# Attention values computed transposed in a hybrid decoder layer, with the reciprocal of the softmax sum spread along columns by transposes

## The chip, the cores and the metric

The kernel runs on one core of a Trainium2 chip. The metric is device time in microseconds of one execution; lower is better. Besides the time there is a profile of one execution. In it PE is TensorE's matmul side and PEld its weight loads, DVE is VectorE, ACT is ScalarE, POOL is GpSimd, and SP is SyncE, which issues most of the transfers.

## The reference

One layer of a decoder, on 512 tokens of 1024 features in float32, and a final RMS norm:

```python
h = rms_norm(x, ffn1_norm[l])
x = x + RES_HALF * swiglu(h, ffn1_w_gate[l], ffn1_w_up[l], ffn1_w_down[l])
h = rms_norm(x, mix_norm[l])
proj = h @ w_in[l]
u, q, k, v = jnp.split(proj, [D_SSM, D_SSM + D_ATTN, D_SSM + D_ATTN + D_KV], axis=-1)
q = partial_rope(...)                     # 8 heads of 64
k = partial_rope(...)                     # 2 heads of 64, v the same
y_ssm = s5_mixer(u, ...)                  # state space part, 512 features, ends in a GLU
y_attn = swa_sink_attention(q, k, v, attn_sinks[l])
y = jnp.concatenate([rms_norm(y_ssm, ssm_out_norm[l]),
                     rms_norm(y_attn, attn_out_norm[l])], axis=-1)
x = x + y @ w_out[l]
h = rms_norm(x, ffn2_norm[l])
x = x + RES_HALF * swiglu(h, ffn2_w_gate[l], ffn2_w_up[l], ffn2_w_down[l])
return rms_norm(x, final_norm)            # after the one layer
```

The attention works in four blocks of 128 tokens; a block sees its own keys and those of the block before it (the first block only its own), under a causal window of 128. Each head has a sink: one more logit in the softmax whose weight is left out of the sum over values.

```python
scores = jnp.where(mask[None, :, None, None], scores, NEG_INF)
probs = jax.nn.softmax(jnp.concatenate([scores, sink], axis=-1), axis=-1)[..., :-1]
out = jnp.einsum('bnkrqs,bnskd->bnqkrd', probs.astype(v.dtype), vw)
```

## The kernel before, in words

Activations are kept transposed: a tile has 128 features on the partitions and the 512 tokens along its columns, so `x` is eight tiles. The large products split weights and activations into a high part of the type fp32r and a rest (`hi`, `lo`), and `mm3` (L199 to L201) issues three matmuls of 512 columns for each pair: hi by hi, hi by lo, lo by hi. A weight arrives by DMA as `wraw`; ACT casts it to `whi` (L162) and DVE subtracts to get `wlo` (L190). The tiles for these three have three buffers each, which come free in the order in which the matmuls are done with them, and two weights are fetched ahead. RMS norms are applied late: a matmul with a column of ones sums the squares by token (`pr`, L244), DVE finds one over the root (`rsqrt`), and two matmuls of ones with two diagonal tiles `dg` (DVE, L265) spread it over the partitions (`prb`, L269); ACT copies that to `R` (L271). What a gained tile needs (`split_gain`) is one ACT op for `hi` (L212) and one DVE op for `lo` (L214).

The layer has three stages: a first feed-forward part, the mixing, and a second feed-forward part. The mixing is a list of steps. The string ORDER holds a letter and a number for each, and a loop runs them in that order; a scheduler then sets each engine's instructions, led by this order and by its own estimate of when inputs are ready. The string ENGINES says for some copies and element-wise operations on which engine they run; what it doesn't name has a default. The steps that matter here, with the tile of 128 tokens (or the half of the heads) as the number:

- `Q` transposes q of one block (`tq`) and makes `qT` from it: ACT the rounded part, and the rest (L1192) on the engine that ENGINES names under `ql`. Where that is POOL, ACT first copies the raw tile out (`qraw`).
- `S` makes the scores of half the heads of a block. DVE adds the mask and takes the row maximum (`mx`, L1394), then has three small operations of four columns: `m`, the maximum with the sink (L1399), `ng`, its negative (L1400), and `ds`, the sink less it (L1401).
- `E` exponentiates with `ng` as bias and the sum as a second result; `den` adds the sink's part, and `rec` is its reciprocal.
- `T` transposes the probabilities (`pt`, L1438), `V` computes the weighted values, `O` what the out-projection needs of them.
- `Y`, `Z`, `G`, `g`, `N0`, `D` are the state space output, its transposes, the GLU, the gate, the rms by token, and the split into `hi` and `lo`. `N1` is the spreading of its rms, named Rs below; `M0` and `M1` are the same for the attention, Ra below.
- `W` and `X` are the two halves of the out-projection (tile `ow`), eight output tiles each with 12 matmuls: `W` takes the state space features, `X` the attention's. `w` multiplies a `W` tile with Rs (`ot`, L1209) and adds it to `x` (L1210, POOL). `x` multiplies an `X` tile with Ra (L1216), adds it to `x` (L1217, DVE), and makes the gained tile for the second feed-forward part (L212, L214).

In `V` the values come out with tokens on the partitions: for each block, head and key block, the transposed probabilities (128 keys by 128 tokens) are the stationary operand and the 64 columns of the head's values are the moving one, so 56 fp32 matmuls (L1455) into `po`, 128 tokens by 8 heads of 64. DVE multiplies with `rec`, spread over a head's 64 columns by a broadcast access pattern, into `ya`; ACT sums its squares by token as a by-product, so that this rms takes no matmul. In `O` PE transposes `ya` (`ty`, L1468, four per block), and ACT and DVE make `ah` and `al`, 128 columns at a time (L1473, L1474).

## Time and profile before

| what | value |
|---|---|
| time, median of three runs (lowest to highest) | 905.81 us (904.67 to 906.43) |
| the profiled execution's own time | 905.8 us |
| its span in the profile | 903.9 us |
| mean granted TensorE clock | 0.996 |
| PE busy | 882.0 us, 98% |
| DVE, ACT, POOL busy | 693.4, 408.1 and 332.9 us |
| bytes moved by DMA | 100.38 MB |

How to read it: the span is the time from the first to the last recorded instruction of the core; the rest of the execution's own time lies around it. Busy times are sums over instructions. PE's is near the span throughout, but matmuls are pipelined and their ends are modelled, so a busy PE may still be waiting in part; what a stage is worth is read from the waits inside it. In rows of a timeline the first number is the start in microseconds from the span's start and the second the duration; a bracket at the end of a row tells how long the engine stood idle before it and what released it.

### The profile page before, as it was taken

How to read it: one execution, taken by the hardware profiler on the slowest of the kernel's cores; microseconds unless marked ns; L12 is line 12 of the kernel's file. 1: busy time of each engine (PE TensorE's matmuls, PEld its weight loads, DVE VectorE, ACT ScalarE, POOL GpSimd, SP SyncE). 2: the span in 40 equal slices, each digit the busy share in tenths (PEclk: the TensorE clock that was granted, in tenths of full speed). 3: DMA queues.
4: the chain of work that ended last, by engine and by line, in shares of the span. 5: the costliest groups of instructions: out<-in, count | busy, mean ns of one | idle time of the engine just before them, and what ended most of it. 6: DMA issues, size and time to landing. Idle time of an engine off the chain costs nothing. (4 is left out here: it accounts for less than half of the span.)

```text
span 903.9 us, 14334 instructions
## 1 busy us (share of the span) xinstructions
PE 882.0 (98%) x5396; PEld 773.7 (86%) x5396; DVE 693.4 (77%) x1253; ACT 408.1 (45%) x768; POOL 332.9 (37%) x295
## 2 busy tenths in 40 slices
PE   9999999999999999999989999999999999999996
PEld 6887888878998898788879887888999889988995
DVE  7998856786995595949887787796798569955966
ACT  7143333323653354612497443552455335533553
POOL 0235227925540450501332153290554055404502
PEclk9999999999999999999999999999999999999999
DMA  7421534455213524456201122223421442144112
GB/s 250 139 83 40 168 121 159 132 157 192 89 36 111 175 87 162 150 176 184 71 1 47 47 94 93 94 70 121 159 88 36 146 152 88 36 127 170 48 48 93
DMA packets 42116, 100.38 MB, mean 111 GB/s; under 512 B 8544, under 2 KB 10816, under 8 KB 41536
## 3 DMA queue, kind: packets, MB, share of 16 engines
q1 hardware_dynamic: 41616, 98.93, 33.9%
q8 instruction: 42, 0.69, 0.3%
q10 hardware_dynamic: 432, 0.55, 0.2%
q14 instruction: 26, 0.21, 0.1%
HBM read 91.63 MB, written 7.83 MB: 110 GB/s over the span
## 5 line engine op out<-in xcount | busy, mean ns | idle before, releaser
L162 ACT CAST whi<-wraw 128x1024 fp32r<-128x1024 f32 (+4 forms) x114 | 101.5, 899 | 210.3 <-PE dn L200 69.8
L190 DVE TENSOR_TENSOR wlo<-wraw,whi 128x1024 fp32r<-128x1024 f32 (+4 forms) x113 | 129.5, 1152 | 35.6 <-ACT whi L162 31.9
L199 PE MATMUL dn<-hi,whi 128*128 128x512 f32 (+1 forms) x336 | 127.5, 386 | 1.1 <-ACT whi L162 1.1
L200 PE MATMUL dn<-lo,whi 128*128 128x512 f32 (+1 forms) x336 | 127.9, 384 | 0.0
L201 PE MATMUL dn<-hi,wlo 128*128 128x512 f32 (+1 forms) x336 | 126.1, 384 | 1.6 <-DVE wlo L190 1.6
L562 POOL TENSOR_TENSOR s<-s,wraw 128x512 f32<-128x512 f32 x52 | 83.2, 1601 | 55.3 <-DVE x L448 35.5
L562 POOL TENSOR_TENSOR s<-wb 128x512 f32<-128x512 f32 x26 | 37.5, 1443 | 168.6 <-DMA wb<-wgs 167.8
L596 DVE TENSOR_TENSOR wlo<-s,whi 128x512 fp32r<-128x512 f32 x104 | 89.1, 898 | 13.2 <-ACT whi L595 12.7
L448 DVE SCALAR_TENSOR_TENSOR x<-dn,x 128x512 f32<-128x512 f32 x56 | 38.3, 688 | 74.0 <-PE dn L201 73.8
L595 ACT CAST whi<-s 128x512 fp32r<-128x512 f32 x104 | 59.3, 619 | 41.6 <-issue 14.9
L199 PE MATMUL gu<-hi,whi 128*128 128x512 f32 x192 | 74.7, 397 | 1.4 <-ACT hi L212 1.3
L199 PEld LDWEIGHTS dn<-hi,whi 128*128 128x128 f32 x336 | 63.1, 188 | 15.0 <-ACT whi L162 2.8
L201 PEld LDWEIGHTS dn<-hi,wlo 128*128 128x128 f32 x336 | 63.0, 188 | 14.5 <-DVE wlo L190 2.0
L200 PE MATMUL gu<-lo,whi 128*128 128x512 f32 x192 | 75.1, 393 | 0.2
L201 PE MATMUL gu<-hi,wlo 128*128 128x512 f32 x192 | 74.3, 390 | 0.0
L200 PEld LDWEIGHTS dn<-lo,whi 128*128 128x128 f32 x336 | 63.1, 188 | 12.1
L286 POOL TENSOR_TENSOR sq<-sq 128x512 f32<-128x512 f32 x17 | 26.0, 1528 | 69.9 <-ACT sq L282 69.8
L596 DVE TENSOR_TENSOR wlo<-wraw,whi 128x512 fp32r<-128x512 f32 x52 | 50.3, 999 | 0.0
L199 PEld LDWEIGHTS gu<-hi,whi 128*128 128x128 f32 x192 | 36.0, 189 | 10.3 <-ACT hi L212 2.0
L200 PEld LDWEIGHTS gu<-lo,whi 128*128 128x128 f32 x192 | 36.3, 189 | 8.8 <-DVE lo L214 1.7
L595 ACT CAST whi<-wraw 128x512 fp32r<-128x512 f32 x52 | 29.2, 615 | 30.0 <-PE dn L200 30.0
L201 PEld LDWEIGHTS gu<-hi,wlo 128*128 128x128 f32 x192 | 36.1, 188 | 7.5
(428 smaller groups left out, 2598.4 us busy)
## 6 DMA issues: line engine op xcount, KB each, us to landing
wraw<-wd SPq DMA_DIRECT2D x48, 384.0 KB, 3.2
wraw<-wgu SPq DMA_DIRECT2D x34, 512.0 KB, 3.5
wb<-wgs SPq DMA_DIRECT2D x52, 256.0 KB, 5.0
wraw<-wgs SPq DMA_DIRECT2D x26, 512.0 KB, 3.5
wraw<-wout SPq DMA_DIRECT2D x8, 512.0 KB, 3.5
x<-xT SPq DMA_DIRECT2D x8, 256.0 KB, 5.1
kV<-mV SPq DMA_DIRECT2D x8, 256.0 KB, 3.2
kC<-mC SPq DMA_DIRECT2D x8, 256.0 KB, 3.1
```

The costliest lines, as they stand in the source:

```text
L162: (e.copy if e is self.nc.scalar else e.tensor_copy)(out, x)
L190: self.eng("lo" + key).tensor_tensor(lo, raw, hi.bitcast(F32), op=ALU.subtract)
L199: mm(out, wh, xh, start=start, stop=False, **kw)
L200: mm(out, wh, xl, start=False, stop=False, **kw)
L201: mm(out, wl, xh, start=False, stop=stop, **kw)
L286: (eng or b.nc.gpsimd).tensor_tensor(self.acc, self.acc, sq, op=ALU.add)
L448: self.added = self.nc.vector.scalar_tensor_tensor(self.x[m], ps, 0.5, self.x[m], op0=ALU.mult, op1=ALU.add)
L562: add = lambda o, x, y: nc.gpsimd.tensor_tensor(o, x, y, op=ALU.add)
L595: self.chained("A", lambda: A.copy(hi[:, c], w))
L596: self.chained("V", lambda: V.tensor_tensor(lo[:, c], w, hi[:, c].bitcast(F32), op=ALU.subtract))
```

## The change

Six things change, all in the mixing stage.

1. **Values.** The values are now the stationary operand (128 keys by 64 features) and the transposed probabilities of two heads the moving one (256 columns), so the result `po` has features on the partitions and tokens along the columns. The heads of the first key-value head go to output rows 0 to 63, those of the second to rows 64 to 127. That is 28 matmuls (L1479 after the change) in place of 56. One `po` tile now holds half the heads of two blocks. The features come out in another order, so the rows of w_out and of the attention's gain are laid out in that order (`ha`) on the way in.
2. **One over the sum.** `rec` would now have to vary along columns. A copy on POOL spreads each block half's `rec` over 64 columns a head (`rx`, eight copies of 256 elements), PE transposes it (`rb`, L1468, four per block, in place of the four of `ya`), ACT copies the result out, and DVE multiplies it with `po` into `ya`, eight operations.
3. **What the out-projection needs.** `O` has no transposes; it makes `ah` and `al` 256 columns at a time, for two blocks at once. The squares (`sa`) are ACT operations of their own with DVE additions, and the rms by token takes eight matmuls with the column of ones, issued among the out-projection's matmuls.
4. **Row maximum.** `m` is gone: `ng` comes in one operation from `mx` and the negated sinks (made once ahead), and `ds` is the sink plus `ng`.
5. **Engines.** `ql1` and `ql3`, four `qT` operations, go from POOL to DVE, and their two `qraw` copies on ACT fall away.
6. **Order.** ORDER is a new one: among others O0 comes before V3 and takes the first two blocks, O1 after it the other two, M0 stands behind O1, N1 before M1, and M1 behind X1. A small tile that `warm_up` makes on POOL, which moves the addresses of the tiles behind it, has 16 columns instead of 32.

```diff
-        m, ng, ds = tiny("m"), tiny("ng"), tiny("ds")
-        V.tensor_tensor(m, mx, sink, op=ALU.max)
-        V.tensor_scalar(ng, m, -1.0, None, op0=ALU.mult)
-        V.tensor_tensor(ds, sink, m, op=ALU.subtract)
+        ng, ds = tiny("ng"), tiny("ds")
+        V.scalar_tensor_tensor(ng, mx, -1.0, self.nsinks[:, half * 4:half * 4 + 4], op0=ALU.mult, op1=ALU.min)
+        V.tensor_tensor(ds, sink, ng, op=ALU.add)
...
         if half == 0:
-            self.rec[b] = self.tp.tile([P, NH], F32, name="rec", bufs=4)
-        V.reciprocal(self.rec[b][:, half * 4:half * 4 + 4], den)
+            self.rec[b] = self.m2(name="rx")
+        rx = self.rec[b][:, half * 256:(half + 1) * 256]
+        self.copy(f"rx{i}", rx.rearrange("p (j v e) -> p v j e", j=2, v=2),
+                  rec.rearrange("p (v j o) -> p v j o", v=2, j=2).broadcast_to([P, 2, 2, HD]), "G")
...
     def values(self, b):
...
-        po = self.ps("po")
-        for n, h in enumerate(HEADS):
...
-                PE.matmul(po[:, n * HD:(n + 1) * HD], pt[:, c:c + P], self.v[:, k0 + kb, kv * HD:(kv + 1) * HD],
-                          start=(kb == 0), stop=(kb == nk - 1))
...
+        ps = self.ps("rb")
+        for k in range(4):
+            PE.transpose(ps[:, k * P:(k + 1) * P], self.rec[b][:, k * P:(k + 1) * P], self.ident)
+        rb = self.m2(name="rb")
+        self.nc.scalar.copy(rb, ps)
+        for half in range(2):
...
             for kb in range(nk):
...
+                for kv in range(2):
+                    pt = self.pts[2 * b + half][kv][:, :2 * nk * P].rearrange("p (j k q) -> p j k q", j=2, k=nk)
+                    PE.matmul(po[kv * HD:(kv + 1) * HD], self.v[:, k0 + kb, kv * HD:(kv + 1) * HD],
+                              pt[:, :, kb], start=(kb == 0), stop=(kb == nk - 1), skip_group_check=True)
+            V.tensor_tensor(ya, po, rb[:, half * 256:(half + 1) * 256].rearrange("p (j q) -> p j q", j=2), op=ALU.mult)
+
+    def attn_out(self, bp):
...
+                hi, lo = (a[:, bp * 256:(bp + 1) * 256] for a in self.attn[k])
+                y = ya[:, j * 256:(j + 1) * 256]
+                nc.scalar.activation(hi, y, AF.Copy, scale=g)
+                nc.vector.scalar_tensor_tensor(lo, y, g, hi.bitcast(F32), op0=ALU.mult, op1=ALU.subtract)
+            sq = self.m2(name="sa")
+            nc.scalar.activation(sq, ya, AF.Square)
```

Three places show how instructions move. Rows have the source line, the operation, output from inputs and the tile; line numbers after the change are a few higher. The first is PE between the last probability transposes and the out-projection (`L199 ow`, after the change `L200 ow`), before:

```order
L1438 MATMUL pt<-cst,pr 128x128 x8
L1455 MATMUL po<-v,pt 128x64 x8
L1438 MATMUL pt<-cst,pr 128x128 x8
L1455 MATMUL po<-v,pt 128x64 x8
L1468 MATMUL ty<-cst,ya 128x128 x4
L1455 MATMUL po<-v,pt 128x64 x4
L1438 MATMUL pt<-cst,pr 128x128 x8
L1455 MATMUL po<-v,pt 128x64 x20
L199 MATMUL ow<-hi,whi 128x512
L244 MATMUL pr<-cst,sq 128x1 x4
L1468 MATMUL ty<-cst,ya 128x128 x4
```

and after:

```order
L1456 MATMUL pt<-cst,pr 128x128 x16
L1468 MATMUL rb<-cst,rx 128x128 x4
L1479 MATMUL po<-pt,v 64x2x128
L1456 MATMUL pt<-cst,pr 128x128 x4
L1479 MATMUL po<-pt,v 64x2x128
L1456 MATMUL pt<-cst,pr 128x128 x12
L1479 MATMUL po<-pt,v 64x2x128 x3
L1468 MATMUL rb<-cst,rx 128x128 x4
L1479 MATMUL po<-pt,v 64x2x128 x11
L1456 MATMUL pt<-cst,pr 128x128 x8
L1468 MATMUL rb<-cst,rx 128x128 x2
```

The values are half as many and stand singly, in threes and in an eleven; the transposes between are of `rb` and come ahead of the values that they scale, where those of `ya` came behind them.

The second place is ACT around the two copies of a spread rms (`R<-prb`), of which the first is the attention's before the change and the state space part's after it. Before:

```order
L162 CAST whi<-wraw 128x1024
L1473 ACTIVATE ah<-ty,gains 128x128 x3
L162 CAST whi<-wraw 128x1024
L271 COPY R<-prb 128x512
L1473 ACTIVATE ah<-ty,gains 128x128
L271 COPY R<-prb 128x512
L162 CAST whi<-wraw 128x1024
L212 ACTIVATE hi<-x_90,gains 128x512
L282 ACTIVATE sq<-x_90 128x512
```

After:

```order
L1492 ACTIVATE ah<-ya,gains 128x256 x2
L1495 ACTIVATE sa<-ya 128x512
L163 CAST whi<-wraw 128x1024
L272 COPY R<-prb 128x512
L163 CAST whi<-wraw 128x1024 x3
L272 COPY R<-prb 128x512
L213 ACTIVATE hi<-x_90,gains 128x512
L283 ACTIVATE sq<-x_90 128x512
```

Three weight casts now stand between the two copies, none right behind the second, and the wider `ah` all stand ahead of the first.

The third is DVE at the same place, from the diagonals of the later spreading (`dg`) through the adds (`ot`, and `x`, whose first tile is x_90). Before:

```order
L265 TENSOR_TENSOR dg<-cst,rb_h 128x512
L265 TENSOR_TENSOR dg<-cst,rb_l 128x512
L190 TENSOR_TENSOR wlo<-wraw,whi 128x1024
L1474 SCALAR_TENSOR_TENSOR al<-ty,gains,ah 128x128
L1209 TENSOR_TENSOR ot<-ow,R 128x512 x2
L1216 TENSOR_TENSOR ot<-ow,R 128x512
L1217 TENSOR_TENSOR x_90<-ot,x_90 128x512
L190 TENSOR_TENSOR wlo<-wraw,whi 128x1024
L214 SCALAR_TENSOR_TENSOR lo<-x_90,gains,hi 128x512
```

After:

```order
L266 TENSOR_TENSOR dg<-cst,rb_h 128x512
L266 TENSOR_TENSOR dg<-cst,rb_l 128x512
L191 TENSOR_TENSOR wlo<-wraw,whi 128x1024 x2
L1219 TENSOR_TENSOR ot<-ow,R 128x512
L1220 TENSOR_TENSOR x_90<-ot,x_90 128x512
L215 SCALAR_TENSOR_TENSOR lo<-x_90,gains,hi 128x512
```

Two weight splits now stand between the diagonals and the first attention add, no `W` tile is multiplied there any more, and none stands between `x` and its `lo`.

80 lines of the change are left out of this document (43 added, 37 removed), and 6 rows, old and new, of the table ORDER.

## The prediction

> **What bounds the kernel now.** I read the page first, then the busy time by stretches, the chain of waits, and last the timeline of each engine around the changed steps. The page says that TensorE (PE) is the engine to watch:
>
> ```profile
> PE 882.0 (98%) x5396; PEld 773.7 (86%) x5396; DVE 693.4 (77%) x1253; ACT 408.1 (45%) x768; POOL 332.9 (37%) x295
> ```
>
> The change touches the mixing stage only, so I cut that stage at the first score matmul (447.98 us), the first GLU matmul (464.67), the first attention add (517.13), and the point in the second feed-forward part where PE takes up the last gained tile (554.25):
>
> ```profile
> core 0: us, PE busy (x) PEld busy (x) DVE busy (x) ACT busy (x) POOL busy (x), PEclk, DMA share, GB/s
> 447.98:464.67 16.69, 13.00 (x91) 10.58 (x89) 16.27 (x85) 14.24 (x44) 6.71 (x6) 1.00 0.11 33
> 464.67:517.13 52.46, 52.08 (x324) 45.54 (x324) 39.39 (x119) 35.06 (x94) 5.71 (x5) 1.00 0.12 41
> 517.13:554.25 37.12, 35.80 (x158) 28.93 (x156) 31.27 (x37) 15.55 (x22) 20.50 (x14) 1.00 0.26 85
> ```
>
> The reader is to see three different limits. In the score stretch VectorE (DVE) is busy 16.27 of 16.69 us and PE only 13.00. In the second PE never rests. The third looks like PE too (35.80 of 37.12), but the chain of waits, here its beginning and end in this region (start, duration, engine, tile, line), says otherwise, and PE's timeline behind it shows why:
>
> ```profile
> 514.75 0.47 PE prb L269 x2
> 515.30 0.59 ACT R L271
> 515.92 0.70 DVE ot L1209
> 516.70 2.57 POOL x L1210 x2
> ...
> 551.73 0.61 DVE ot L1216
> 552.43 1.02 DVE x L1217
> 553.48 0.73 ACT hi L212
> ```
>
> These are the two ends of PE's wait:
>
> ```profile
> 542.72 0.39 PE L201 MATMUL ow<-ah,wlo 128*128 128x512 f32 x1
> 554.25 0.73 PE L199 MATMUL gu<-hi,whi 128*128 128x512 f32 x2 [1.27 <-ACT hi L212]
> ```
>
> PE ends the out-projection at 542.72, runs twelve microseconds of feed-forward matmuls on tiles 0 to 6, and then stands 1.27 us for tile 7, which DVE and ScalarE (ACT) are still making. So the time of this region is: when the broadcast 1/rms that the adds need is ready (514.75), plus a chain of eight adds on DVE of some 39 us. A PE saving ahead of 514.75 shortens the kernel by moving that chain's start; one behind it buys only a longer wait. After 554.25 nothing is edited, and I count 0 there.
>
> **PE work from the first GLU matmul to the broadcast.** The rows for the pitches:
>
> ```profile
> 489.50 4.58 PE L1455 MATMUL po<-v,pt 128*128 128x64 f32 x40
> 444.28 0.45 PE L1304 MATMUL py<-matT,U 128*64 128x128 f32 x4
> 447.61 0.44 PE L1305 MATMUL py<-matC,S 128*64 128x128 f32 x4
> 890.05 0.61 PE L1571 MATMUL prb<-dg,cst 128*128 128x256 f32 x2
> 494.61 0.95 PE L244 MATMUL pr<-cst,sq 128*128 128x1 f32 x8
> 443.32 1.03 PE L1182 MATMUL tq<-cst,q 128*128 128x128 f32 x8
> 515.75 0.39 PE L199 MATMUL ow<-hi,whi 128*128 128x512 f32 x1
> 518.25 0.39 PE L201 MATMUL ow<-hi,wlo 128*128 128x512 f32 x1
> ```
>
> Values today: 112 passes (56 fp32 matmuls, two passes each); 40 of them take 4.58 us, less a modelled tail of 0.27, so 0.11 us each and 12.4 in all. New: 28 matmuls, 56 passes of 256 columns into 64 output rows. No row has that shape. Upper bound: L1571, 256 columns at full width, 0.61 less a tail of 0.38: 0.23 a pass, 13.1 us. Lower: the 64-row tiles of L1304/L1305, which alternate between two halves of the array: 15 groups of 4 from 444.28 to 447.61, so 0.0555 us for 128 columns; for 256 twice that, 0.11, 6.2 us. I take the lower, since the new matmuls too alternate between output rows 0 to 63 and 64 to 127: **-6.3**. The order shows two of them alone and groups of 3 and 11, where one has no partner (4 x 2 x 0.12 = 1.0), and seven changes into the half-width shape (443.32 to 444.28 is 0.96 us for eight transposes of 0.11: 0.09 each time, 0.6): **+1.5**. Eight rms matmuls are new, 16 passes; L244 shows (0.95 - 0.24)/7 = 0.10: **+1.7**. Sixteen transposes of `rec` replace sixteen of `ya`: 0. Four probability transposes move from before the first GLU matmul to behind it: **+0.4**. And the order counts: before, 72 out-projection matmuls stand ahead of the broadcast (Rs) that starts the adds; now the SSM's Rs comes early and the adds wait for the attention's Ra, behind 96. The 12 from 515.75 to 518.25 are 0.227 apart: 24 x 0.227 = **+5.4**. Sum **+2.7**: the saving on values is more than spent on a later broadcast.
>
> **The score stretch.** It is DVE's:
>
> ```profile
> L1399 DVE TENSOR_TENSOR m<-mx,gains 128x4 f32<-128x4 f32 x8 | 3.0, 374 | 0.0
> L1400 DVE TENSOR_SCALAR ng<-m 128x4 f32<-128x4 f32 x8 | 2.8, 355 | 0.0
> L1192 DVE TENSOR_TENSOR qT<-tq,qT 64x512 fp32r<-64x512 f32 x4 | 2.8, 688 | 2.4 <-ACT qT L1191 2.4
> 452.05 5.36 POOL L1192 TENSOR_TENSOR qT<-qraw,qT 64x512 fp32r<-64x512 f32 x4 [5.01 <-DVE mx L1394]
> 452.22 1.13 DVE L1399 TENSOR_TENSOR m<-mx,gains 128x4 f32<-128x4 f32 x1
> 463.63 0.15 DVE L1399 TENSOR_TENSOR m<-mx,gains 128x4 f32<-128x4 f32 x1
> L1332 POOL TENSOR_TENSOR yl<-y,yh 128x256 fp32r<-128x256 f32 x3 | 2.3, 771 | 8.4 <-DVE y L162 6.7 <-DVE ds L1401 1.7
> ```
>
> The same four-column maximum takes 0.15 us alone and 1.13 while GpSimd (POOL) works on `qT`. The 16 ops of m and ng take 5.8; alone they would take 16 x 0.15 = 2.4, so 3.4 of it is stretching. Removed are this and m's own 8 x 0.15: 4.6. Added: four `qT` on DVE, 2.8. That is -1.9 at best. But POOL gets eight `rx` copies of 256 elements, whose length no row shows; bounded by 0 and by the 0.77 of `yl`, they are up to 6.2 us in which small DVE ops may be stretched again. Four `qT` on POOL cost 3.4 that way, so the worst is -1.9 + 3.4 = +1.5. I take **-1.2**: the copies are spread out, and half of them fall outside this stretch. ACT loses two raw copies here, which is slack.
>
> The Trainium skill, SBUF — State Buffer, section "Who interferes with whom", says that a VectorE instruction with two SBUF inputs contends with a GpSimd instruction that reads SBUF, and that the later one is blocked completely. The 1.13 beside the 0.15 agrees. By that rule each `rx` copy stops whichever of `ng`, `ds`, `den`, `yl` meets it for its whole length, and the sum would use +1.5 here in place of -1.2.
>
> **Cover that is lost.** With 4 us less PE filler before the first out-projection matmul, PE can reach it before the gained SSM tiles are ready. Today that wait is small:
>
> ```profile
> 494.27 0.50 PE L199 MATMUL ow<-hi,whi 128*128 128x512 f32 x1 [0.19 <-ACT hi L212]
> 475.10 1.11 DVE L1349 TENSOR_TENSOR y<-y,sg 128x512 f32<-128x512 f32 x1 [1.70 <-ACT sg L1343]
> 485.81 1.28 ACT L1417 ACT_TABLE_LOAD   x1 [1.71 <-DVE ds L1401]
> ```
>
> ACT and DVE have idle of 1.7 us in that path themselves, and ACT's own list gets shorter: 16 small `ah`, four squares and two raw copies go; eight wider `ah`, four `rb` copies and four squares come. Bounds 0 and 2; I take **+0.6**. The DMA queue on SP is unchanged row for row; on POOL the SSM sums now queue behind `rx` copies, whose inputs are ready earlier.
>
> **From the broadcast to the first attention add.** Before, it runs from the first `prb` at 514.59 through R, two `ot` and the next `ot` at 517.13: 2.54 us. Now R(Ra) stands on ACT behind a third weight cast, and DVE has the split of that weight ahead of the add. That cast waits for the out-projection that frees its buffer, as this one did:
>
> ```profile
> 518.49 1.05 ACT L162 CAST whi<-wraw 128x1024 fp32r<-128x1024 f32 x1 [2.60 <-PE ow L200]
> 519.90 1.22 DVE L190 TENSOR_TENSOR wlo<-wraw,whi 128x1024 fp32r<-128x1024 f32 x1
> ```
>
> The buffer frees about when the broadcast starts: cast 1.05, then split 1.2, so some 2.2 us: **-0.3**.
>
> **The chain of adds.**
>
> ```profile
> 517.13 0.68 DVE L1216 TENSOR_TENSOR ot<-ow,R 128x512 f32<-128x512 f32 x1
> 519.29 0.69 DVE L1217 TENSOR_TENSOR x<-ot,x 128x512 f32<-128x512 f32 x1 [1.48 <-POOL x L1210]
> 521.04 0.74 DVE L214 SCALAR_TENSOR_TENSOR lo<-x,gains,hi 128x512 fp32r<-128x512 f32 x1
> 550.98 0.75 DVE L214 SCALAR_TENSOR_TENSOR lo<-x,gains,hi 128x512 fp32r<-128x512 f32 x1 [0.79 <-ACT hi L212]
> ```
>
> The first add waits 1.48 us for POOL's SSM add; with Rs early that is done long before. Six weight splits stand in the chain today, four in the new order. The two that left filled time in which `lo` would wait 0.79 for `hi`, so each saves 1.2 - 0.8 = 0.4 net; at best, if POOL overlaps fall kindly, 1.5 each. So -2.2, at best -4.5, at worst -0.7 (one split gone, the POOL wait taken by another). I take **-2.3**.
>
> **How the numbers follow.** +2.7 - 1.2 + 0.6 - 0.3 - 2.3 = -0.5. The profiled execution took 905.8 us with a span of 903.9, and the median of the three runs is 905.81, so the sum may stand on either: **905.3 us**. What a measurement tells from no change is about 0.2%, 1.8 us: faster is below 904.0, slower above 907.6. The forecast is no change that can be measured.
>
> **The rivals.** (a) *The chain shortens by its best case*: -4.5 there, -1.9 in the scores, no lost cover: 2.7 - 1.9 - 0.3 - 4.5 = -4.0, 901.8. For it, `x` on DVE takes 1.02 late in the chain beside 0.69 early, so there is something to win; against it, the same POOL sums run beside the chain. Chance 0.24. (b) *PE sets the pace after all*, the chain keeps ahead: values -6.3 + 1.5 + 1.7, scores -1.2, the wait of 1.27 gone: -5.6, 900.2. It needs a chain four microseconds shorter than I find, though the adds' own bound, -4.5, is as large: 0.11. (c) *Slower: POOL's copies stall DVE in the score stretch*: decided where an `rx` copy lasts over about 0.5 us, so that eight of them reach the block that `qT` was; +1.5 in place of -1.2 and the GLU inputs later: -0.5 + 2.7 = +2.2, 908.0. For it the 1.13, against it that PE has work beside it: 0.18. (d) *Slower: the halves do not overlap*: 0.23 a pass, +6.9, 912.2; against it L1304: 0.06. My forecast: 0.41.
>
> The Trainium skill, TensorEngine Tiling (Array Packing), "Key Properties", states that a change of tiling mode drains the array; it gives no price, the 0.09 above is this trace's, and should each of the seven drains cost as much as one full 0.27 tail, (d)'s side would gain 1.3 us.
>
> (a) and (b) give 0.35 of faster, and the forecast's lower edge 0.05: 0.40. (c) and (d) give 0.24, and its upper edge 0.03: 0.27. Same: 0.33. Eight in ten I put at 900.0 to 908.5: (a), (b) and (c) lie inside, (d) and the tails beyond (b) and (c) outside; since both signs hold much of the chance, the forecast's own range is 903.5 to 907.5.
>
> **What would show it.** Right: the values' 56 passes take about 0.11 us each; `m` is gone and DVE's `ng` near 0.15; the last `prb` before the adds stands about 2 us later against the first score; the tile-7 wait of PE grows from 1.27 to some 4 us. Wrong: passes at 0.23; `ng` or `ds` near 1 us beside `rx`; a chain from first `ot` to the last `hi` of well under 33 us or over 36.5; or PE not waiting at tile 7 at all.

## The result and the profile after

The changed kernel took 911.29 us (median of five runs, 909.97 to 913.71), the kernel before 905.51 (904.67 to 906.43) beside it: 1.0067 times as long, with a 95% interval of 1.0049 to 1.0085. That is slower by more than the 0.2% that a measurement tells from no change. It lies 6.0 us above the forecast and outside the range; my forecast of no change was wrong, and the time moved to the side on which I had put less than on the other.

The profiled execution has a span of 909.5 us, 5.6 more than before. TensorE's (PE's) row on the page, first, tells nothing of it:

```profile
PE 881.9 (97%) x5356; PEld 766.8 (84%) x5356; DVE 694.5 (76%) x1248; ACT 407.4 (45%) x758; POOL 331.7 (36%) x299
```

The busy time by stretches does. The first three rows are the changed kernel in the prediction's three stretches (first score matmul, first GLU matmul, first `ot` of an attention add, PE taking tile 7 in the second feed-forward part). The last two cut the first two anew, at the first out-projection matmul (493.65) and at the last broadcast (521.46). The columns are as in the prediction: stretch, length, then busy time of PE, PEld, DVE, ACT and POOL with the instruction counts, granted clock, DMA.

```profile
446.55:462.45 15.90, 12.58 (x84) 11.23 (x84) 14.60 (x70) 12.60 (x41) 1.81 (x3) 0.90 0.10 33
462.45:523.66 61.21, 57.88 (x314) 43.89 (x313) 45.50 (x129) 37.84 (x90) 11.32 (x13) 1.00 0.13 43
523.66:558.80 35.14, 30.86 (x133) 23.96 (x131) 28.48 (x35) 13.50 (x20) 17.93 (x12) 1.00 0.24 76
...
446.55:493.65 47.10, 40.45 (x246) 31.15 (x247) 39.22 (x146) 37.49 (x107) 9.61 (x14) 0.96 0.10 34
493.65:521.46 27.81, 27.81 (x144) 22.16 (x143) 19.74 (x52) 11.44 (x21) 3.52 (x2) 1.00 0.12 39
```

The kernel before, cut at the same two events:

```profile
447.98:494.27 46.29, 42.22 (x295) 36.75 (x293) 38.72 (x150) 38.71 (x113) 11.98 (x10) 1.00 0.11 36
494.27:514.59 20.32, 20.32 (x107) 17.29 (x108) 15.73 (x51) 10.01 (x23) 0.00 (x0) 1.00 0.15 52
```

| stretch | before | after | change | predicted |
|---|---|---|---|---|
| first score matmul to first GLU matmul | 16.69 | 15.90 | -0.8 | -1.2 |
| to the first out-projection matmul | 29.60 | 31.20 | +1.6 | -2.7 |
| to the last broadcast before the adds | 20.32 | 27.81 | +7.5 | +6.0 |
| to the first attention `ot` | 2.54 | 2.20 | -0.3 | -0.3 |
| to tile 7 in the second feed-forward part | 37.12 | 35.14 | -2.0 | -2.3 |
| sum | 106.27 | 112.25 | +6.0 | -0.5 |

(The prediction's terms are put in the stretch in which they fall: of its +2.7, the values' -6.3 + 1.5 = -4.8, probability transposes of +0.4 and reciprocal transposes of +1.1 lie ahead of the out-projection, together with the +0.6 of lost cover, and +1.7, +5.4 and -1.1 behind it.) The stretches outside, where nothing is edited, give back 0.4: 0.2 at the start, 1.2 where a drop of the clock was absent (the last section), less 1.1 behind tile 7. Of that, 0.7 lies between tile 7 and the first matmul into `gua` behind the down-projection (276.25 us in place of 275.55); the profiles of the kernel before and of its edits that leave the addresses alone show 274.7 to 276.3 there.

Two rows of the table fail. Ahead of the out-projection PE has less work, 40.45 us in place of 42.22, and yet takes longer: its standing grew from 4.07 us (46.29 - 42.22) to 6.65. The lower clock at its beginning (0.90 up to the first GLU matmul) is not the reason: with Ra behind W3, an experiment below that leaves this part alone, the clock there is 1.00, and the stretch is 47.10 us again, with 39.53 of work and 7.57 of standing. What it stood for, the view of waits says (engine, line, who released it: total, times, longest):

```profile
PE sc L1406 <- DVE qT L1195: 1.8, 4, 0.6
PE sc L1406 <- ACT y L163: 1.6, 1, 1.6
PE pt L1456 <- ACT rb L1470: 1.0, 1, 1.0
PE glu L200 <- DVE mx L1411: 0.8, 1, 0.8
PE po L1479 <- DVE pt L163: 0.6, 1, 0.6
```

There is no one culprit: scores, transposes, GLU and values each wait for a different tile from DVE or ACT. Behind the out-projection's start PE never rests, and 27 more of its matmuls stand ahead of the broadcast. The changed kernel's timelines around that broadcast and around the last tiles, first DVE's, then PE's:

```profile
516.54 0.68 DVE L266 TENSOR_TENSOR dg<-cst,rb_l 128x512 fp32r<-128x512 f32 x1
523.66 0.69 DVE L1219 TENSOR_TENSOR ot<-ow,R 128x512 f32<-128x512 f32 x1
524.45 0.69 DVE L1220 TENSOR_TENSOR x<-ot,x 128x512 f32<-128x512 f32 x1
```

```profile
489.85 2.80 PE L1479 MATMUL po<-pt,v 128*64 128x256 f32 x22
...
521.46 0.62 PE L270 MATMUL prb<-dg,ones_r 128*128 128x512 f32 x2
...
552.28 0.73 PE L200 MATMUL gu<-hi,whi 128*128 128x512 f32 x2 [1.62 <-ACT hi L213]
555.54 0.73 PE L200 MATMUL gu<-hi,whi 128*128 128x512 f32 x2 [1.28 <-ACT hi L213]
558.80 0.73 PE L200 MATMUL gu<-hi,whi 128*128 128x512 f32 x2 [1.28 <-ACT hi L213]
```

The diagonals are ready at 517.22 (516.54 + 0.68), but PE takes the broadcast at 521.46, 4.2 us later, because it stands that far down PE's list. And PE then waits 1.62 + 1.28 + 1.28 = 4.2 us for tiles 5, 6 and 7, where it waited 1.27 before, for tile 7 alone: DVE's chain, from the first `ot` on, sets the end.

### The profile page after: what moved, and what is told of

Its sections match the earlier page's. It is cut to its first block, busy times and chain, and to the rows that moved or that the text cites. A ratio compares the mean times of both kernels' runs of the same rounds, so it can differ in the third digit from the quotient of the medians.

```text
span 909.5 us, 14239 instructions
## 1 busy us (share of the span) xinstructions
PE 881.9 (97%) x5356; PEld 766.8 (84%) x5356; DVE 694.5 (76%) x1248; ACT 407.4 (45%) x758; POOL 331.7 (36%) x299
## 3 DMA queue, kind: packets, MB, share of 16 engines
q1 hardware_dynamic: 41616, 98.93, 34.1%
## 4 chain that ended last, share of the span: by engine, by line
PE 83%; DVE 10%; issue 2%; ACT 2%; DMA 1%; POOL 0%; SPq 0%; DVEq 0%; ACTq 0%; POOLq 0%
PE dn L202 7%; PE dn L200 7%; PE dn L201 7%; PE gu L200 7%; PE gu L201 7%; PE gu L202 7%; PE gua L202 5%; PE gua L200 5%; PE gua L201 5%; PE guc L202 3%; PE guc L200 3%; PE guc L201 3%; DVE wlo L597 1%; PE gub L202 1%; PE pt L1145 1%
## 5 line engine op out<-in xcount | busy, mean ns | idle before, releaser
L200 PE MATMUL dn<-hi,whi 128*128 128x512 f32 (+1 forms) x336 | 127.4, 386 | 0.5 <-ACT whi L163 0.5
L597 DVE TENSOR_TENSOR wlo<-s,whi 128x512 fp32r<-128x512 f32 x104 | 85.1, 859 | 15.7 <-ACT whi L596 15.3
L200 PE MATMUL gu<-hi,whi 128*128 128x512 f32 x192 | 74.7, 397 | 4.4 <-ACT hi L213 4.2
L200 PEld LDWEIGHTS dn<-hi,whi 128*128 128x128 f32 x336 | 63.1, 188 | 14.4 <-ACT whi L163 2.3
L597 DVE TENSOR_TENSOR wlo<-wraw,whi 128x512 fp32r<-128x512 f32 x52 | 53.6, 1063 | 0.0
L200 PEld LDWEIGHTS gu<-hi,whi 128*128 128x128 f32 x192 | 35.8, 188 | 14.5 <-ACT hi L213 6.0
```

Source lines behind the costliest of these rows:

```text
L200: mm(out, wh, xh, start=start, stop=False, **kw)
L597: self.chained("V", lambda: V.tensor_tensor(lo[:, c], w, hi[:, c].bitcast(F32), op=ALU.subtract))
```

## The experiments

My theory after the result: (1) the kernel is slower because the adds start later; (2) the saving on values, ahead of the out-projection, is worth nothing, because something else sets when the out-projection can start. The rivals were the new copies and waits (`rx`, `rb`, `qT` on DVE), the new order of the front, and the addresses. "Before" and "after" in a label's text say which kernel was edited; times are medians, with the ratio to the kernel before beside it.

### Is a late start of the adds enough?

**The kernel before with its last broadcast later.** Rs moves behind twelve out-projection matmuls and nothing else is touched:

```diff
-X0 W4 N1 w2 W5 w0
+X0 W4 W5 N1 w2 w0
```

> The kernel before with N1 (and w2, which needs it) behind W5. On TensorE the broadcast that starts the adds then stands behind 84 out-projection matmuls and not 69, 15 x 0.227 = 3.4 us later, with its inputs long ready, so that TensorE doesn't wait for it. Theory (the start of the adds sets the end of the region): tile 7 comes 3 us later or more against the first out-projection matmul (63 us and not 60.0), and the kernel loses 2.5 to 3.5 us. Rival (another chain sets the end, as where the changed kernel's broadcast came 2.7 us earlier and tile 7 only 0.7): tile 7 comes less than 1 us later, and the time stays within 1 us of before.

Measured: 911.71 us, 1.0063 (1.0044 to 1.0083). PE's and DVE's timelines of this kernel, whose first out-projection matmul is at 493.04:

```profile
516.73 0.63 PE L266 MATMUL prb<-dg,ones_r 128*128 128x512 f32 x2
518.33 0.50 PE L196 MATMUL ow<-ah,whi 128*128 128x512 f32 x1 [0.97 <-ACT R L268]
...
558.80 0.73 PE L196 MATMUL gu<-hi,whi 128*128 128x512 f32 x2 [1.28 <-ACT hi L209]
```

```profile
523.39 0.69 DVE L1214 TENSOR_TENSOR x<-ot,x 128x512 f32<-128x512 f32 x1
```

The broadcast comes 23.7 us after the first out-projection matmul (20.3 before), the first add 30.35 (25.02), tile 7 65.76 (59.98). This one move, with values, sums and front as they were, costs as much as the whole change. The first half of the theory held, but the loss is twice the 2.5 to 3.5 us expected: the broadcast moved by 3.4 us and the first add by 5.3, because a weight split now stands ahead of that add on DVE and itself waits 1.40 us for ACT's cast.

**The kernel before with that broadcast earlier**, Rs behind Ra:

```diff
-M1 O3 W3 X0 W4 N1 w2
+M1 N1 O3 W3 X0 W4 w2
```

> The kernel before with N1 right behind M1. On TensorE the last of the four broadcast matmuls then stands behind 48 out-projection matmuls and not 69, 4.8 us earlier in the list; VectorE had its diagonal ready at 510.6 us, 4 us before TensorE took it up, so TensorE may wait 2 us for an earlier one. Theory (the start of the adds sets the end of the region, both ways): the first add comes 2.5 us earlier or more against the first out-projection matmul, tile 7 comes 2 us earlier (58.0 and not 60.0), and the kernel gains 2 us, to 903.5. Rival (the chain of adds is held by later out-projection tiles once it starts earlier, or TensorE's wait lowers its clock): tile 7 comes within 1 us of 60.0 or later, and the kernel gains nothing.

Measured: 909.24 us, 1.0028 (1.0012 to 1.0044). The broadcast was 2.0 us earlier, but PE stood 2.47 us for its diagonals, and then the adds had nothing to add. DVE's timeline, where `ow` is the first attention tile of the out-projection:

```profile
521.31 0.69 DVE L1213 TENSOR_TENSOR ot<-ow,R 128x512 f32<-128x512 f32 x1 [3.96 <-PE ow L198]
```

The first add came 2.0 us later (27.01), tile 7 3.2 later. So the rival held: the broadcast stood where its own inputs and the first tile came together. It was no test of an earlier first add, then; the place of the broadcast alone does not set it.

**The changed kernel with Ra earlier.** At 517.22 the diagonals are ready. Two earlier places:

```diff
-W2 W3 X0 W4 w2 W5 w0 X1 M1 X2
+W2 W3 M1 X0 W4 w2 W5 w0 X1 X2
```

> The changed kernel with one step moved in ORDER: M1 (the attention's rms spread) stands behind W3 and not behind X1. In the written order its last broadcast matmul then stands behind 66 out-projection matmuls and not 96. Theory (the adds start too late, because the broadcast stands too far back): the last broadcast comes 30 x 0.227 = 6.8 us earlier against the first out-projection matmul, TensorE's three waits of 1.3 to 1.6 us at the gained tiles 5, 6 and 7 vanish, and the kernel gains 4 us (907.3 from 911.3). Rival (the adds themselves set the pace, and start no earlier because VectorE has other work there): the first add comes at most 2 us earlier, some of the three waits stay, and the gain is under 1.5 us.

Measured: 919.77 us, 1.0151 (1.0133 to 1.0169). PE's timeline at the broadcast, and the busy time behind it:

```profile
517.75 0.76 PE L270 MATMUL prb<-dg,ones_r 128*128 128x512 f32 x1 [4.34 <-DVE dg L266]
```

```profile
517.70:523.40 5.70, 5.65 (x14) 4.49 (x15) 1.70 (x3) 0.00 (x0) 2.52 (x2) 0.51 0.00 1
```

PE stood 4.34 us for the diagonals and then worked at a granted clock of 0.51 for 5.7 us. The place was too early: its own new wait spoils it as a test. Behind W4 there is none:

```diff
-X0 W4 w2 W5 w0 X1 M1 X2
+X0 W4 M1 w2 W5 w0 X1 X2
```

> The changed kernel with M1 (the attention's rms spread) behind W4 in ORDER. On TensorE its two broadcast matmuls then stand behind 72 and 84 out-projection matmuls, not both behind 96; VectorE had the diagonals ready at 516.6 and 517.2 us, and TensorE took the broadcast up at 521.46. Theory (the place of the broadcast in TensorE's order starts the adds late): the second broadcast matmul comes 12 x 0.227 = 2.7 us earlier against the first out-projection matmul, TensorE waits up to 0.6 us for the first one, the three waits at gained tiles 5 to 7 shrink together by 2 us or more, and the kernel gains 2.2 us (909.1). Rival (the adds' own chain sets the end): the stretch from the first add to tile 7 grows by what is won ahead, and the gain is under 0.5 us.

Measured: 911.14 us, 1.0064 (1.0052 to 1.0076), not to be told from the change. PE's timeline:

```profile
519.51 0.40 PE L267 MATMUL prb<-dg,ones_r 128*128 128x512 f32 x1
...
558.67 0.73 PE L197 MATMUL gu<-hi,whi 128*128 128x512 f32 x2 [1.29 <-ACT hi L210]
```

The broadcast moved as it should, the first add came 2.5 us earlier, and tile 7 only 0.65 (counted from the first out-projection matmul): the chain stretched from 34.35 to 36.18 us. Starting the adds earlier in the changed kernel gained no time. DVE's timeline shows two of its operations beside POOL's adds:

```profile
535.05 2.32 DVE L188 TENSOR_TENSOR wlo<-wraw,whi 128x1024 fp32r<-128x1024 f32 x1
537.29 1.77 DVE L212 SCALAR_TENSOR_TENSOR lo<-x,gains,hi 128x512 fp32r<-128x512 f32 x1
```

They take 1.2 and 0.75 elsewhere. Is that the reason? Then taking POOL's adds away, to DVE, on top of the last edit, should bring the gain back:

```diff
-"pt51=V y001=A ...
+"pt51=V w0=V w1=V w2=V w3=V w4=V w5=V w6=V w7=V y001=A ...
```

> The changed kernel with M1 behind W4 and, beside that, the eight adds of the state space part (w) on VectorE and not on GpSimd. Theory (GpSimd's adds stretch VectorE's operations in the chain of adds: x takes 1.23 us on the mean and 0.69 alone, a weight split 1.40 and 1.21 alone): x falls to under 1.0, the stretch from the first add to tile 7 falls from 36.2 by 2 us or more, and the kernel gains 2 us against M1 behind W4 alone (909.1), though VectorE has 8 x 0.69 us more to do. Rival (VectorE is full there): the stretch grows by up to 3 us, and so does the time.

Measured: 911.77 us, 1.0062 (1.0047 to 1.0078). The stretching went: `x` takes 0.84 us on the mean in place of 1.23, a weight split 1.22 in place of 1.44, and from the first attention add to tile 7 the chain takes 34.12 us (525.04 to 559.16) in place of 36.18, as the theory had it. But that add comes 1.1 us later, behind two `W` adds that DVE now makes first. So tile 7 comes only 0.9 us earlier, and the time (1.0062 beside 1.0064) doesn't show it. POOL's adds are thus one reason why the chain is longer behind the earlier start. By DVE's groups the other is a fifth weight split in it: the splits there take 7.2 us, four of them 4.9 in the changed kernel, and the eight `lo` 7.0 in place of 6.2.

Taken together (us from the first out-projection matmul; the time against the kernel before of the same runs):

| kernel | first add | tile 7 | tile 7 against before | time against before |
|---|---|---|---|---|
| before | 25.02 | 59.98 | | |
| Rs behind Ra | 27.01 | 63.14 | +3.2 | +3.6 |
| after, Ra behind W4, `w` on DVE | 29.45 | 63.57 | +3.6 | +6.0 |
| after, Ra behind W4 | 28.32 | 64.50 | +4.5 | +5.7 |
| after | 30.79 | 65.14 | +5.2 | +5.8 |
| before, Rs behind W5 | 30.35 | 65.76 | +5.8 | +6.3 |
| after, Ra behind W3 | 30.11 | 71.49 | +11.5 | +13.7 |

Tile 7 follows the first add by 34.1 to 36.2 us, save in the last, where the clock dropped, and time follows tile 7 roughly: an edit of the changed kernel also has its longer front (0.8 us), and the one with `w` on DVE lost another 1.4 us behind tile 7 in its profile. Later adds lengthened the kernel; no edit here made it shorter by earlier ones.

### Was the saving on values ever worth time?

**The kernel before with fewer values.** Its values leave out the earlier key block where there are two, so 24 of 56 value matmuls are gone with the order kept:

```diff
-            for kb in range(nk):
+            for kb in range(nk - 1, nk):
...
-                          start=(kb == 0), stop=(kb == nk - 1))
+                          start=True, stop=True)
```

> The kernel before with less work in the weighted values: those over the previous block's keys are left out, 24 of the 56 matmuls, 48 passes of 0.11 us, 5.3 us of TensorE, 40 of the passes ahead of the first out-projection matmul (4.4 us). The output lacks their part. Theory (TensorE doesn't set the pace between the first score and the out-projection; another chain lies just below it, so that what is saved on values there becomes waits): that stretch falls from 46.3 by less than 1.5 us, and the kernel gains less than 2 us. Rival (TensorE sets it, as the prediction summed it): it falls by 4 us or more, and the kernel gains 3 us or more, since the adds start earlier by as much.

Measured: 910.43 us, 1.0048 (1.0032 to 1.0063). With less work the kernel is slower. From the first score to the first out-projection matmul it takes 46.27 us, where 46.29 were taken before: PE's work there went from 42.22 to 38.39, its standing from 4.07 to 7.88. PE's timeline and busy time at the end of that stretch:

```profile
487.97 2.34 PE L1452 MATMUL po<-v,pt 128*128 128x64 f32 x20
492.73 0.80 PE L196 MATMUL ow<-hi,whi 128*128 128x512 f32 x1 [2.42 <-ACT hi L209]
496.20 0.63 PE L197 MATMUL ow<-lo,whi 128*128 128x512 f32 x1
496.63 0.63 PE L198 MATMUL ow<-hi,wlo 128*128 128x512 f32 x1
```

```profile
492.73:501.00 8.27, 8.27 (x35) 7.41 (x36) 6.21 (x14) 5.29 (x13) 0.00 (x0) 0.60 0.01 2
```

All that PE saved it waits for the state space part's `hi`; and the wait of 2.42 us is followed by 8 us at a granted clock of 0.60, with matmuls 0.43 us apart (496.20 to 496.63), which puts the broadcast 2.35 us later. This settles the second half of the theory for the kernel before: with the rest as it is, work taken from PE ahead of the out-projection is worth nothing. That it costs something goes with the clock, whose mean over an execution is 0.986 to 0.994 in the six of this kernel and 0.994 to 0.998 in those of the kernel before beside it.

**What sets that start?** Late in ACT's list ahead of `hi` stand the last four exponentials (E7). Their first one and the end of that list in ACT's timeline of the kernel before, and the first one in that of the kernel with fewer values:

```profile
487.10 0.51 ACT L1417 ACTIVATE pr<-s,ng 128x256 f32<-128x256 f32 x1
...
493.24 0.37 ACT L1473 ACTIVATE ah<-ty,gains 128x128 fp32r<-128x128 f32 x1 [0.42 <-DVE al L1474]
493.50 0.71 ACT L212 ACTIVATE hi<-y,gains 128x512 fp32r<-128x512 f32 x1
```

```profile
485.56 0.51 ACT L1414 ACTIVATE pr<-s,ng 128x256 f32<-128x256 f32 x1
```

Counted from the first score matmul it begins at 39.1 us before and, with fewer values, at 39.1 again (485.56 - 446.46): ACT does not get there sooner when PE has less to do. Behind the exponentials come squares and the first block's four `ah`, three of which wait 0.42 to 0.48 us each, two of them for DVE's `al`, and only then the `hi` that the out-projection needs. In the changed kernel E7 begins at 40.5 us (487.07), the out-projection does not wait for `hi`, and PE works from 483.4 us to its start without a wait. So I moved the last scores and exponentials (S7, E7) behind E6, in the kernel before, in the same with fewer values, and in the changed one with Ra behind W4:

```diff
-E6 T1 G0 ... T3 S7 E7 g3
+E6 S7 E7 T1 G0 ... T3 g3
```

> The kernel before with two steps moved: S7 and E7, the scores and the softmax of the last half block, stand behind E6 and not among the GLU steps. ScalarE then has all exponentials in one run: one table load of 1.28 us fewer, and no wait of 1.7 us for VectorE's ds behind the last one. TensorE's work is the same. Theory (ScalarE's list, with VectorE's maximum ahead of it, sets when the out-projection can begin; taking 4.3 us of TensorE's work away moved nothing): the stretch from the first score to the first out-projection matmul falls from 46.3 by 1.5 us or more, and the kernel gains 1 us or more. Rival (neither engine's sum sets it; the waits move to the next late input): it stays within 0.7 us of 46.3, and the time within 0.9 us of before.

> The kernel before with both: the values over the previous block's keys left out (4.3 us of TensorE ahead of the out-projection; the output lacks them) and S7 and E7 behind E6 (one table load and a wait less on ScalarE). Theory (two chains, TensorE's list and that of ScalarE with VectorE, are about equally long there, so that shortening one alone moves nothing): together they shorten the stretch from the first score to the first out-projection matmul from 46.3 to 44.5 us or less. Rival (a third chain holds it, or what is taken from one list comes back as a lower clock): it stays above 45.6.

> The changed kernel with S7 and E7 behind E6 and M1 behind W4. Theory (ScalarE's list bounds the front here too, and with its second table load gone TensorE's saving on values can show): the stretch from the first score to the first out-projection matmul falls from 47.1 to 45.5 or less, and the time from 911.1 (M1 behind W4 alone) to 909.5 or less. Rival (the new chain of rx, rb and ya holds it): it stays within 0.7 us of 47.1, and the time at 911.

Measured: 906.73 (1.0005, 0.9992 to 1.0017), 909.01 (1.0030, 1.0017 to 1.0044) and 914.01 us (1.0080, 1.0062 to 1.0099). The stretch to the out-projection became 47.91, 46.59 and 51.70 us: no shorter in any (the last with a clock of 0.90 behind the first GLU matmul), so the exponentials are not the one thing that sets the start. Cut at the first GLU matmul, the kernel before shows more:

| kernel before, with | to the first GLU matmul | to the out-projection |
|---|---|---|
| nothing else | 16.69 | 29.60 |
| fewer values | 16.68 | 29.59 |
| S7, E7 early | 19.03 | 28.89 |
| both | 19.05 | 27.54 |

The scores of S7 now lengthen the first part by 2.3 us. In the second, with E7 out of the way, PE works without a rest (28.89 of 28.89), and now fewer values shorten it, by 1.35 us, where they gained 0.01 before; then PE stands 2.0 us for ACT's `hi` again. That fits two lists of about equal length, PE's and ACT's, but both of these profiles have a clock of 0.94 in that part, so how much each is worth alone stays open, as it does for the changed kernel.

**The division left out.** If `rx`, the reciprocal's transposes and their copy are what PE waits for in the changed kernel, it gains without them:

```diff
-        rx = self.rec[b][:, half * 256:(half + 1) * 256]
-        self.copy(f"rx{i}", ...)
...
-            PE.transpose(ps[:, k * P:(k + 1) * P], self.rec[b][:, k * P:(k + 1) * P], self.ident)
-        self.nc.scalar.copy(rb, ps)
...
-            V.tensor_tensor(ya, po, rb..., op=ALU.mult)
+            V.tensor_copy(ya, po)
```

> The changed kernel without the spreading of one over the sum: no rx copies, no rb transposes and copies, and ya is a plain copy of po, so the output lacks the division. Theory (this chain itself makes the waits): the stretch from the first score to the first out-projection matmul loses the 14 transposes in it, 1.7 us, and the waits of 0.6 and 1.1 us that the rb tile and its copy end, so it falls from 47.1 to 43.7 or less, and the kernel gains 3 us or more. Rival (the chain costs only its own work on TensorE, the waits move to the next late input): it falls by at most 1.9 us, and the kernel gains at most 1.9.

Measured: 910.73 us, 1.0060 (1.0048 to 1.0072). Sixteen transposes, four copies on ACT and eight on POOL are gone, and the stretch ahead of the out-projection is 46.31 us, 0.8 shorter and as in the kernel before, with 39.32 of work and 6.99 of standing (39.53 and 7.57 with the clock at 1.00). The rival held: the spreading of the reciprocal is not what made the kernel slower.

**The order of the front, and `qT`.** The changed kernel with the order of before up to V3 (O0 behind D1, since it takes two blocks), and with `ql1` and `ql3` on POOL again:

```diff
-... Q2 q3 Y1 S4 S0 Q1 Q3 S1 S2 E0 Z0 E1 ... V3 O1 W0 M0 W1 N1 ...
+... Q2 q3 Y1 S0 S4 Q1 Q3 S1 S5 E0 Z0 E4 ... V3 O1 W0 M0 W1 N1 ...
```

> The changed kernel with the order of before from its first step to V3 (O0 behind D1), and the new order behind that. Theory (TensorE's waits between first score and out-projection, 6.7 us in place of 4.1, come from the new order of scores, softmax and GLU steps): the stretch from the first score matmul to the first out-projection matmul falls from 47.1 by 2.6 to about 44.5 us, and the kernel gains up to 2.6 us. Rival (they come from the new chain itself, rec to rx to rb to its copy to ya, and from the PSUM tiles it holds): the stretch stays within 0.7 us of 47.1, and the time within 1 us of 911.3.

```diff
-"pt51=V y001=A ...
+"pt51=V ql1=G ql3=G y001=A ...
```

> The changed kernel with ql1 and ql3 back on GpSimd, so that four of the eight qT operations leave VectorE. Theory (VectorE, loaded with four more qT, makes the scores late, and TensorE's waits from the first score to the broadcast grow from 4.1 to 6.7 us because of it): these waits fall to about 4.1 and the kernel gains 2.5 us (908.8). Rival (the waits come from the new order of scores, softmax and state space tiles, or from the rx copies on GpSimd): the waits stay near 6.7 and the time within 0.9 us of 911.3, or it rises by up to 1.5 us, because GpSimd stretches the small operations of VectorE again.

Measured: 914.58 (1.0102, 1.0087 to 1.0116) and 914.32 us (1.0093, 1.0073 to 1.0113). The old order makes the front 50.62 us with 9.72 of standing; the new order fits the new values better, and my theory that it did harm fell. With `qT` on POOL the front is 46.51 us with 7.40 of standing, and the waits for `qT` are not fewer: 1.0 us less for DVE's, and a new row in the view of waits for POOL's:

```profile
PE sc L1406 <- POOL qT L1195: 1.8, 2, 1.2
```

That theory fell too: the kernel gained nothing. Its time says little more, since the profile is that of its slowest execution (917.27 us; the other five took 912.1 to 915.2), with a clock of 0.64 at 880 to 884 us and 0.51 at 884 to 888, far from the edit.

### The small parts alone

On the kernel before: `qT` of blocks 1 and 3 on DVE (`ql1=G ql3=G` taken out of ENGINES); `ng` in one operation without `m`, with `warm_up`'s tile at 64 columns so that the other tiles keep their place; and the changed kernel's order from W0 on.

```diff
-"pt51=V ql1=G ql3=G y001=A ...
+"pt51=V y001=A ...
```

> The kernel before with ql1 and ql3 on VectorE, that edit alone. Theory (four more qT on VectorE make the scores late): TensorE's waits between the first score and the out-projection grow by 2 to 2.5 us and the kernel loses 2 us (907.5 from 905.5). Rival, as in the prediction (GpSimd's qT stretch m and ng by 3.4 us and four qT cost 2.8): m and ng fall to 0.15 us each and the kernel gains up to 0.6 us.

```diff
-        V.tensor_tensor(m, mx, sink, op=ALU.max)
-        V.tensor_scalar(ng, m, -1.0, None, op0=ALU.mult)
-        V.tensor_tensor(ds, sink, m, op=ALU.subtract)
+        V.scalar_tensor_tensor(ng, mx, -1.0, self.nsinks[:, half * 4:half * 4 + 4], op0=ALU.mult, op1=ALU.min)
+        V.tensor_tensor(ds, sink, ng, op=ALU.add)
```

> The kernel before with the row maximum as in the change: m is gone, ng and ds come from mx and the negated sinks; qT stays on GpSimd, and the size of warm_up's small tile is set so that the large tiles stay where they were. Theory (VectorE's chain lies below TensorE's in the score stretch): m's 3.0 us and part of the stretching of ng go, the stretch from the first score to the first out-projection matmul falls by 1.5 us or more, and the kernel gains 1 to 2 us. Rival (the stretch doesn't follow VectorE's sum either): it falls by less than 0.7 us, and the time stays within 0.9 us of 905.5.

```diff
-V3 W0 M0 O1 W1 O2 W2 M1 O3 W3 X0 W4 N1 w2 W5 w0 X1 X2 X3 X4 W6 x0 ...
+V3 W0 M0 O1 W1 N1 O2 W2 O3 W3 X0 W4 w2 W5 w0 X1 M1 X2 X3 X4 x0 ...
```

> The kernel before with the new order from W0 on (N1 behind W1, M1 behind X1, W6 late; O2 and O3 where O1 and O2 stood), that edit alone. On TensorE the broadcast that starts the adds stands behind 78 out-projection matmuls and not 69, 2.0 us later. Theory (the new tail costs time by itself: the adds start later and the chain behind them is not shorter by as much): the kernel loses 1.5 us or more. Rival (the prediction's terms: what the broadcast loses, 2.0, the shorter way to the first add and the weight splits that left the chain win back, 0.3 + 2.3): within 0.9 us of 905.5.

Measured: 907.0 (1.0005, 0.9994 to 1.0016), 906.7 (1.0017, 1.0004 to 1.0030) and 915.0 us (1.0105, 1.0087 to 1.0123). The first two gain nothing and lose less than 0.2%. What they do to DVE's small operations, by the groups of the score stretch of the first and of the second:

```profile
L1400 DVE TENSOR_SCALAR ng<-m 128x4 f32<-128x4 f32 x6 | 1.5, 243 | 0.1
L1399 DVE TENSOR_TENSOR m<-mx,gains 128x4 f32<-128x4 f32 x6 | 0.9, 154 | 0.0
```

```profile
L1398 DVE SCALAR_TENSOR_TENSOR ng<-mx,nsinks 128x4 f32<-128x4 f32 x6 | 2.7, 458 | 0.0
L1399 DVE TENSOR_TENSOR ds<-gains,ng 128x4 f32<-128x4 f32 x6 | 2.9, 480 | 0.0
```

In the same stretch of the kernel before, `m` takes 0.446 us on the mean, `ng` 0.421 and `ds` 0.149. Without POOL's `qT`, `m` is short (0.154) and `ng` shorter (0.243). Where POOL's `qT` stays and only `m` goes, the stretching does not go with it: `ng` takes 0.458, and `ds` 0.480. The third is inconclusive: with the old values PE stood 4.51 us ahead of the state space part's broadcast, and the clock was 0.51 and 0.64 in the two stretches of 2 us behind it, so this order was not seen alone.

### The addresses

`warm_up`'s tile went from 32 to 16 columns, which moves every tile behind it by 64 bytes. The changed kernel with 32, and the kernel before with 16:

```diff
-        self.shift(self.tp, 16)
+        self.shift(self.tp, 32)
```

> The changed kernel with the small tile of warm_up at 32 columns again, so that all tiles made after it stand where they stood. Theory (the addresses don't matter): within 0.9 us of 911.3, and TensorE still gives 0.05 us more to each pair of products in the second feed-forward part's gated stretches than in the kernel before. Rival (this 1.1 us in all comes from the addresses): it vanishes, and the kernel gains 1.1 us.

> The kernel before with the small tile of warm_up at 16 columns, that edit alone. With 32 columns the changed kernel's down-projection matmuls take 229.0 ns each and not 226.7. Theory (what counts is where the tiles behind it stand, and the changed kernel's small tiles moved that by the same 64 bytes that the edit takes back): here the edit moves them off their place, the matmuls take 229 ns, and the kernel loses 3 to 4.5 us. Rival (16 columns are better in any case): 226.7 ns or less, and the time within 0.9 us of 905.5, or below.

Measured: 915.71 us (1.0116, 1.0096 to 1.0136) and 912.63 us (1.0083, 1.0068 to 1.0097). The addresses do matter: both edits lose, the second more than its 3 to 4.5 us. PE's timelines in the first feed-forward part, first the changed kernel, then it with 32, then the kernel before with 16; the rows are those of the same weight operand and lie twelve, twelve and nine matmuls apart:

```profile
299.58 0.39 PE L200 MATMUL dn<-hi,whi 128*128 128x512 f32 x1
...
302.30 0.39 PE L200 MATMUL dn<-hi,whi 128*128 128x512 f32 x1
```

```profile
299.30 0.39 PE L200 MATMUL dn<-hi,whi 128*128 128x512 f32 x1
...
302.05 0.39 PE L200 MATMUL dn<-hi,whi 128*128 128x512 f32 x1
```

```profile
299.92 0.40 PE L199 MATMUL dn<-hi,whi 128*128 128x512 f32 x1
...
302.02 0.39 PE L199 MATMUL dn<-hi,whi 128*128 128x512 f32 x1
```

A matmul of 512 columns takes 2.72/12 = 0.227 us in the changed kernel, as in the kernel before, 2.75/12 = 0.229 with its tile at 32, and 2.10/9 = 0.233 in the kernel before with 16. In the built programs the `hi` and `lo` tiles, which move through PE here, start at a multiple of 256 bytes in the kernel before and in the changed one, 64 bytes past one in the changed one with 32, and 192 past one in the kernel before with 16; the weights' `whi` and `wlo` start at such a multiple in all four. The new tiles of the change alone would have moved them: the 16 in `warm_up` puts them back, and is worth 915.71 - 911.29 = 4.4 us. The rival that the loss comes from addresses falls with it.

## Why the prediction was wrong

**The step that failed** is "PE work from the first GLU matmul to the broadcast", in what it made of the values: it booked the 4.8 us that they save as time because "in the second PE never rests" (52.08 of 52.46 busy). The values did become shorter, by nearly as much as I said; the stretch from the GLU to the out-projection became 1.6 us longer, where the terms made it 2.7 shorter. The step "Cover that is lost" was there to catch this, with +0.6 and a bound of 2, read from idle times of ACT and DVE in the profile of before. Without it the terms made the stretch 3.3 us shorter, so they miss by 4.9. Of this, 2.9 is standing, which grew from 0.38 to 3.33 us. The other 2.0 is work that was not saved: 0.9 of the values, 0.5 in the 48 GLU matmuls, which come 0.248 us apart in place of 0.237 at a granted clock of 1.00, and some 0.6 whose place is open. Against the first score, the last broadcast came 8.3 us later and not the "about 2" that I gave as a sign of being right.

A removal on the kernel before, of no new instruction at all, lost its whole 3.8 us in waits. A PE that is busy 99% of a stretch can still be in step with another engine whose list ends there at the same time. The small wait of 0.19 at the end of that stretch, which I quoted, was the sign that both arrived together, and I read it as a small exposure; with 24 value matmuls fewer it was 2.42. In the changed kernel itself no run took the values away, so that they bought waits there too is read from its standing and not from a test.

**Mis-sized.** The broadcast comes 7.5 us later behind the first out-projection matmul, not 6.0. Not 24 but 27 more out-projection matmuls stand ahead of it (69 before, 96 after), worth 22.71 - 16.25 = 6.5 us by their starts; the 16 rms matmuls of the attention take 1.6, the values left behind that point 0.4 more, and the transposes there give back 1.0. The sign was right and the rest of the change would have had to pay for it. That a broadcast so late is enough for such a loss, the kernel before with Rs behind W5 shows; that the changed kernel would be fast without it is not shown, since the one clean test of an earlier broadcast there moved the first add by 2.5 us and gained nothing.

**Right.**

- The values' shape. 22 passes take 2.80 us less a last pass of 0.38, over 21: 0.115 each (I said 0.11 with lone ones extra). All value passes, by their starts, take 8.5 us in place of 12.4, so -3.9 against -4.8 (of which 0.1 is a slip: 12.4 less 6.2 is 6.2 and not 6.3). Rival (d), that the halves do not overlap, is false, though its time of 912.2 came nearest.
- From the broadcast to the first attention `ot`: 2.20 us (521.46 to 523.66), forecast 2.2.
- The chain of adds: 2.0 us shorter, forecast 2.3, and PE's waits there 4.2 us, forecast "some 4", though at tile 7 alone and not spread over tiles 5 to 7. That part of the mechanism, an end set by DVE's chain and not by PE, is what the later broadcast acted through.
- The copies on POOL. Their group and `ng`'s, from the changed kernel's groups by shape:

```profile
L163 POOL COPY rx<-rec 128x256 f32<-128x256 f32 x8 | 3.6, 452 | 22.7 <-DVE ds L1417 18.4 <-DVE rec L1438 4.4
L1416 DVE SCALAR_TENSOR_TENSOR ng<-mx,nsinks 128x4 f32<-128x4 f32 x8 | 1.2, 156 | 0.1
```

  An `rx` copy takes 0.45 us, under the 0.5 that I set for rival (c), and `ng` 0.156. Rival (c) is false, and the score stretch shortened by 0.8 of the 1.2 forecast. But this gain, too, lies ahead of the out-projection, where it bought nothing: `qT` on DVE and the row maximum without `m`, each alone on the kernel before, gained no time.

**The rivals and the range.** Of the slower cases none had the mechanism that came: each made a new operation long. The case that was missing is the simplest, that the saving comes to nothing and the later broadcast stays: with the terms as I had them, and nothing for values, transposes, scores and cover ahead of the out-projection, 6.0 - 2.6 = +3.4, or 909.2 us, already above the range. `warm_up`'s 16 columns, 4.4 us by themselves, I left out of the sum; that it was right to is luck.

**What stays open.** How much of the waits ahead of the out-projection each list on PE, ACT and DVE makes in the changed kernel. The new values under the old order of the out-projection were not tried alone, since two blocks now share a tile; so it is not shown that the change without its new order would have gained.

## What to carry to other kernels

Before a saving on a full engine is booked as time, find what the next stage waits for besides it, and try the saving by leaving work out: a run that drops 24 matmuls and gains nothing says in one look what no busy share does. Where a serial chain ends a stage, price a new order first by the place of its first link in each engine's list: here 27 matmuls ahead of one broadcast, 6.5 us, were the largest term. And do not expect the reverse for nothing: a start moved 2.5 us earlier was eaten by the chain behind it. When an edit adds or drops tiles, look at the pitch of a matmul that was not edited, since addresses alone moved this kernel by 4 to 7 us.
